# The third pair of heads projected one tile at a time, and a straighter pace for attention

## The chip, the cores and the metric

One core of a Trainium2 chip runs the whole kernel. Its engines are TensorE (PE; its weight loads are PEld), VectorE (DVE), ScalarE (ACT), GpSimd (POOL) and SyncE (SP, which here only issues DMAs). Each engine works through its own list of instructions, and they wait for each other by semaphores. The metric is the device time of the kernel in microseconds (us), the median of several executions; lower is better. A profile is one execution recorded instruction by instruction.

## The reference, cut to what matters

An encoder block: a normalised input goes through one input projection, whose columns feed a Mamba-2 branch (z, xBC, dt) and an attention branch (q, k, v); both are normalised, projected out, and followed by a SwiGLU feed-forward.

```
h = rms_norm(x, pre_mix_gain)                    # 1024 rows x 1024
z, xbc, dt_raw, q, k, v = split(h @ w_in)
xbc = silu(causal_depthwise_conv(xbc))           # -> ssd_scan(...) * silu(z), group rms_norm
# stick-breaking attention, 8 heads of 64, strictly causal
log_1mb = log_sigmoid(-z);  after = reverse exclusive cumsum(log_1mb)
w = exp(log_sigmoid(z) + after);  o = w @ v      # rms_norm per head
x = x + rms_norm(concat(y_ssd, y_sb) @ w_out)
x = x + rms_norm((silu(h2 @ w_gate) * (h2 @ w_up)) @ w_down)
```

## The kernel before, in words

Every large product is made as three matmuls (`mm3`, lines 78 to 80): operands are split in a high and a low part (`split`, line 74 a cast on ACT, line 75 a subtraction on DVE), and high x high, low x high and high x low are summed in PSUM. A tile of the input projection is 128 columns of `w_in` against all 1024 rows: two halves of 512 rows, each 8 x 3 matmuls of 128x512, 48 in all (`proj`, names `pj_q`, `pj_k`, `pj_v`, `pj_x`, `pj_z`). Heads go in pairs: one q, one k and one v tile for two heads; pair 0 is made before the stage of this case, pairs 1, 2 and 3 are `qkv1`, `qkv2`, `qkv3`. The eight x tiles (`conv_tile`) are scaled into `u` (line 375) and convolved by `taps` (line 384 three times and line 387 once, on DVE).

In the stage of this case two streams are merged into one program: attention (a list of 32 units: pair, head, two blocks of 128 queries) and the fill (the projection tiles in the order of `PLAN`, with `taps` and the chunked scan `ssd` as side work between their steps). Each step of a stream states costs, PE time for the fill and DVE time for attention. The merge compares attention's share of its total with a curve over the fill's share and lets the one that is behind go on:

```
x = min(f / F_ALL * 8, 7.99)
pace = PACE[int(x)] + (x - int(x)) * (PACE[int(x) + 1] - PACE[int(x)])
if not da and (db or (not stall and a / A_ALL <= pace)):
    c = next(ga, None)
```

So `PACE` has nine points, one for each eighth of the fill. A scheduler then orders each engine's list; an engine takes its list in order.

A unit of attention: `zp` (line 565 and 566, q against high and low k), two sigmoids on ACT into `sn` and `sp` (lines 567 and 568), a select on POOL (line 570), on DVE a running product (`sn`, line 571) and a product (`sp`, line 572), four transposes a piece on PE (`tp`, line 582), the cast `wh` on ACT and the rest `wl` on DVE (lines 586, 587), and the product with v (`o`, line 594). After the last unit of a pair its output is squared on ACT and summed on PE (`nps`, line 491).

Before attention's first sigmoids ACT makes eight decay tiles `ab` (line 362; each comes from a DMA, a POOL select in line 360 and a DVE subtraction in line 361) and, after the last of them, the scales that the sigmoids take (lines 366 and 367). v of pair 0 is transposed on PE (`pv`) and copied (`vv`, line 549 on ACT, line 550 on DVE). The weights of a tile are fetched from DRAM in two halves of 256 KB (`wr`, line 168) some matmuls into the tile before, and split into `wh` and `wl`; two raw buffers and four split ones are shared by all tiles.

Of the kernel before, what the change touches and what calls it, by code (L numbers as in the profile page):

```python
# [32 lines left out]
EPS = 1e-6  # L33
NEG = -1e30

PLAN = ('qkv1', 'x0', 'x1', 'x2', 'x3', 'x4', 'x5', 'qkv2', 'x7', 'x6', 'ssd', 'qkv3', 'z0', 'z1', 'r0', 'z2', 'z3', 'wo', 'l1', 'o0')

PACE = (-0.109, 0.104, 0.264, 0.337, 0.474, 0.601, 0.751, 0.876, 1.027)
A_ALL, F_ALL = 146.4, 259.0
SIDE = 1  # L40
URGENT = 150
# [7 lines left out]
def tile_hybrid_block(  # L49
# [20 lines left out]
    last_mm, evac, last_dve = [None], [None], [None]  # L70
# [6 lines left out]
    def mm3(ps, ah, al, bh, bl, start, stop, more=False):  # L77
        T.matmul(ps, lhsT=ah, rhs=bh, start=start, stop=False, skip_group_check=more)  # L78
        T.matmul(ps, lhsT=ah, rhs=bl, start=False, stop=False, skip_group_check=more)  # L79
        last_mm[0] = T.matmul(ps, lhsT=al, rhs=bh, start=False, stop=stop, skip_group_check=more)  # L80
# [9 lines left out]
    def psum(tag, name, shape=None, dt=F32):  # L90
        return psP.tile(shape or [P, 512], dt, tag=tag, name=name, bufs=BANKS[tag])
# [81 lines left out]

    ORDER = [f"{k}{t[3]}" if t[:3] == "qkv" else t for t in PLAN if t[0] in "qxz" for k in ("qkv" if t[0] == "q" else "x")]
    START = {"q": COL_Q, "k": COL_K, "v": COL_V, "x": COL_XBC, "z": COL_Z}
    cols = [(n, START[n[0]] + P * int(n[1])) for n in ["q0", "k0", "v0"] + ORDER]
    w_tiles = {}

    def fetch_w(half=None):

        if cols:
            name, col = cols[0]
            w = w_tiles.setdefault(name, [])
            for dh in range(2) if half is None else (half,):
                w.append(load_w_half(col, name, dh))
            if len(w) == 2:
                cols.pop(0)

    def w_of(w, d):
        hi, lo = w[d // 4]
        return hi[:, d % 4, :], lo[:, d % 4, :]
# [5 lines left out]
    with tc.tile_pool(reuse_waits="tile", name="xp", bufs=4, side="left") as xp:  # L199
# [5 lines left out]
        for d in range(ND):  # L205
            t = xp.tile([P, S], F32, tag="xt", name=f"xt{d}")
# [38 lines left out]
    def proj(name, evac, dve):  # L245
        if name not in w_tiles:
            fetch_w()
        w = w_tiles.pop(name)
        for n in range(2):
            ps = psum("mm", f"pj_{name}")  # L250
            for d in range(ND):
                mm3(ps, *w_of(w, d), hh[d][n], hl[d][n], d == 0, d == ND - 1)
                if n == 0 and d in (3, 5):
                    fetch_w(d // 2 - 1)
                if d % 2 and d < ND - 1:
                    yield 1.3, 0
            evac(n, ps, slice(512 * n, 512 * n + 512))
            yield 1.3, dve

    def qkv_tiles(j, st):  # L260


        def store(key, n, i, t):
            nc.sync.dma_start(qkv_d[j][key][i][:, 512 * n : 512 * n + 512], t)

        def two(key, n, src):
            hi, lo = [t2.tile([P, 512], F32R, tag="t2", name=key + x) for x in "hl"]
            split(hi, lo, src)
            store(key, n, 0, f32(hi))
            store(key, n, 1, f32(lo))  # L270

        def evac_q(n, ps, sl):
            two("q", n, ps)
            st["q"] = n == 1

        def evac_k(n, ps, sl):
            kr = t2.tile([P, 512], F32, tag="t2", name="kr")
            V.tensor_tensor(kr, ps, R_b[:, sl], ALU.mult)
            two("k", n, kr)
            st["k"] = n == 1  # L280

        def evac_v(n, ps, sl):
            vr = t2.tile([P, 512], F32, tag="t2", name="vr")
            V.tensor_tensor(vr, ps, R_b[:, sl], ALU.mult)
            if j == 0:
                v_first.append(vr)
            else:
                store("v", n, 0, vr)
            if n == 1:
                st["v"] = True  # L290

        return evac_q, evac_k, evac_v

    v_first = []

    def proj_qkv(j, st):
        for key, evac in zip("qkv", qkv_tiles(j, st)):
            yield from proj(f"{key}{j}", evac, {"q": 0.6, "k": 1.2, "v": 0.6}[key])


    def dt_stage():
# [68 lines left out]
    def conv_tile(c):  # L370
        u = big.tile([P, S + 3], F32, tag="u", bufs=2, name=f"u{c}")
        G.memset(u[:, S : S + 3], 0.0)

        def evac(n, ps, sl):
            V.tensor_tensor(u[:, sl], ps, R_b[:, sl], ALU.mult)

        yield from proj(f"x{c}", evac, 0.6)

        def taps():
            y = big.tile([P, S], F32, tag="G", name=f"cy{c}")  # L380
            sg = big.tile([P, S], F32, tag="dec", name=f"csg{c}")
            A.activation(y, u[:, 3 : 3 + S], AF.Identity, scale=cw[:, 0, c : c + 1], bias=cb[:, c : c + 1])
            for j in (1, 2, 3):
                V.scalar_tensor_tensor(y, u[:, 3 - j : 3 - j + S], cw[:, j, c : c + 1], y, ALU.mult, ALU.add)
                yield 0, 1.2
            A.activation(sg, y, AF.Sigmoid)
            V.tensor_tensor(y, y, sg, ALU.mult)
            nc.sync.dma_start(cx_d[c], y)
            yield 0, 1.1

        side.append(taps())
# [268 lines left out]
    def merge(ga, gb):  # L660
# [3 lines left out]
        while not (da and db):  # L664
# [3 lines that stand above are left out]
# [10 lines left out]
    st = [dict() for _ in range(4)]  # L678
# [33 lines left out]
    wo = rpA = None  # L712
# [94 lines left out]
    def stage(t):  # L807
        nonlocal wo
        if t[:3] == "qkv":
            yield from proj_qkv(int(t[3]), st[int(t[3])])  # L810
        elif t[0] == "x":
            yield from conv_tile(int(t[1]))
        elif t == "ssd":
            side.append(ssd())
            yield 0, 0.1
        elif t[0] == "z":
            if t == "z0":
                yield from flush()
            yield from z_tile(int(t[1]))
        elif t == "wo":  # L820
            right_h.close()
            wo = es_w.enter_context(tc.tile_pool(reuse_waits="tile", name="wo", bufs=1, side="right"))
            out_load(0, "early")
            raws = fetch_wo()
            yield 0, 3
            yield from load_wo(raws)
            rows_rstd(1, 1, t2, tag="t2")
            yield 0, 1
        elif t == "r0":
            rows_rstd(1, 0, t2, tag="t2")  # L830
            yield 0, 1
        elif t == "o0":
            yield from out_mm(0, "early")
        elif t == "l1":
            out_load(1, "early")
            yield 0, 3

    def fill():
        for t in PLAN:
            for c in stage(t):  # L840
# [494 lines left out]
    for i in range(n_all):  # L1335
        while len(steps) <= min(i + AHEAD, n_all - 1):
            steps.append(prep(len(steps)))
        q, p = "1267543"[i // NP], i % NP
        if p == 0 and q in "1675":
            banks[q] = [bank("pd") for _ in range(4)]  # L1340
        if q == "3" and p >= NP - TAIL:
# [3 lines left out]
            for b in range(4):  # L1345
                for t in range(TAIL - 1, -1, -1):
                    mms(i - t, b)
                t = temp()
# [10 lines left out]
        for b in range(4):  # L1359
# [15 lines left out]
            elif q == "4":  # L1375
                t = temp()
# [44 lines left out]
```

## Time and profile before

| | us |
|---|---|
| median of 3 runs | 1226.1 (1224.39 to 1229.47) |
| the profiled execution's own time | 1223.84 |
| its span, first to last instruction | 1222.1 |
| PE busy | 1186.1 (97%) |
| DVE busy | 929.8 (76%) |
| ACT busy | 585.3 (48%) |

"Busy" is the union of an engine's instructions; a matmul that waits for its operands inside the pipeline counts as busy, so a busy PE isn't PE at its peak. The profiled execution lies 2.26 us under the median, and its span 1.74 us under its own time.

### The profile page before, as it was taken

Reading aid. Unit: us, or ns where it says so; the run is one execution under the profiler, and the core shown is the slowest. Engines: PE = TensorE matmul, PEld = TensorE weight load, DVE = VectorE, ACT = ScalarE, POOL = GpSimd, SP = SyncE. Lnnn points to the kernel's source line nnn. Section 1 sums busy time; section 2 is a strip of 40 time slices with the busy share of each in tenths; the row PEclk is TensorE's granted clock in tenths of the full one; section 3 lists DMA queues with packets and bytes.
Section 4 is the critical chain, followed back from the end, with each engine's and each line's share of the span. In section 5 each row is a group of like instructions: output and inputs, shape, how many; then the busy total and the mean of one; then the engine's idle time right before and its main releaser. Section 6 shows DMA issues by size and latency. Waiting matters only on the chain.

```text
span 1222.1 us, 16315 instructions
## 1 busy us (share of the span) xinstructions
PE 1186.1 (97%) x5641; PEld 966.0 (79%) x5641; DVE 929.8 (76%) x1461; ACT 585.3 (48%) x1115; POOL 92.6 (8%) x232
## 2 busy tenths in 40 slices
PE   9998999999999998999999999999999999999997
PEld 7776778887887776788788888888888888888885
DVE  7478988769997978668898755566555558998877
ACT  7347655546654776446653323333233335444453
POOL 0041110010100100011200000000000000000000
PEclk9999999999999999999999999999999999999999
DMA  6793342345657424767973322322223298233346
GB/s 192 198 341 111 92 134 91 118 118 172 180 151 221 137 79 155 227 191 221 314 207 110 104 77 79 104 69 87 78 78 104 96 334 285 69 122 100 114 136 236
DMA packets 141994, 184.27 MB, mean 151 GB/s; under 512 B 10724, under 2 KB 96964, under 8 KB 141912
## 3 DMA queue, kind: packets, MB, share of 16 engines
q1 hardware_dynamic: 130656, 152.23, 40.8%
q0 software_dynamic: 7424, 25.17, 5.5%
q10 hardware_dynamic: 3832, 5.84, 1.3%
q8 instruction: 44, 0.72, 0.3%
q14 instruction: 38, 0.31, 0.1%
HBM read 133.28 MB, written 49.92 MB: 150 GB/s over the span
## 4 chain that ended last, share of the span: by engine, by line
PE 72%; DVE 13%; DMA 5%; ACT 5%; issue 4%; SPq 1%; DVEq 0%; ACTq 0%
PE pd L79 5%; PE pd L78 5%; PE pd L80 5%; DVE sn L571 3%; DMA Rb<-r_d 2%; PE o L594 2%; PE tp L582 2%; PE pj_x L78 2%; PE pj_x L80 2%; PE pcu L80 2%; PE pcg L80 2%; PE peu L80 2%; PE peg L80 2%; PE peu L79 2%; PE peg L79 2%
## 5 line engine op out<-in xcount | busy, mean ns | idle before, releaser
L74 ACT CAST flhi<-fraw 128x512 fp32r<-128x512 f32 x98 | 60.3, 621 | 153.5 <-PE pcg L79 35.6
L79 PE MATMUL pd<-folo,fohi 128*128 128x512 f32 x260 | 101.4, 390 | 0.0
L80 PE MATMUL pd<-fohi,folo 128*128 128x512 f32 x260 | 101.2, 389 | 0.0
L78 PE MATMUL pd<-fohi 128*128 128x512 f32 x260 | 101.2, 389 | 0.0
L571 DVE TENSOR_TENSOR_SCAN sn<-sn,smask 128x1024 f32<-128x1024 f32 (+3 forms) x64 | 87.3, 1365 | 17.6 <-ACT sn L567 17.4
L75 DVE TENSOR_TENSOR fllo<-fraw,flhi 128x512 fp32r<-128x512 f32 x98 | 66.7, 684 | 29.2 <-ACT flhi L74 29.2
L567 ACT ACTIVATE sn<-zp,msc 128x512 f32<-128x512 f32 (+2 forms) x96 | 56.0, 585 | 34.5 <-PE zp L566 28.9
L74 ACT CAST fohi<-rt 128x512 fp32r<-128x512 f32 x83 | 48.5, 618 | 45.6 <-PE pd L79 22.9
L586 ACT CAST wh<-tp 128x512 fp32r<-128x512 f32 (+1 forms) x80 | 42.7, 544 | 38.5 <-PE tp L582 38.0
L74 ACT CAST flhi<-fs 128x512 fp32r<-128x512 f32 x44 | 27.3, 622 | 69.5 <-PE peg L79 34.5
L75 DVE TENSOR_TENSOR folo<-rt,fohi 128x512 fp32r<-128x512 f32 x83 | 54.9, 687 | 7.3 <-ACT fohi L74 7.3
L587 DVE TENSOR_TENSOR wl<-tp,wh 128x512 fp32r<-128x512 f32 (+1 forms) x80 | 49.7, 628 | 10.8 <-ACT wh L586 10.3
L79 PEld LDWEIGHTS pd<-folo,fohi 128*128 128x128 f32 x260 | 48.8, 188 | 10.6 <-DVE folo L75 0.6
L568 ACT ACTIVATE sp<-zp,msc 128x512 f32<-128x512 f32 (+2 forms) x96 | 55.9, 585 | 2.5 <-PE tp L582 2.4
L78 PEld LDWEIGHTS pd<-fohi 128*128 128x128 f32 x260 | 48.8, 188 | 10.2
L80 PEld LDWEIGHTS pd<-fohi,folo 128*128 128x128 f32 x260 | 48.8, 188 | 10.1
L582 PE MATMUL tp<-ident,sp 128*128 128x128 f32 x288 | 48.0, 278 | 5.7 <-DVE sp L572 5.1
L78 PE MATMUL po<-woh,yhl 128*128 128x512 f32 x128 | 50.5, 395 | 2.6 <-ACT yhl L74 2.2
L1015 POOL DMA_DIRECT2D a_d<-sg x44 | 23.9, 542 | 376.8 <-DVE sg L1014 376.8
L78 PE MATMUL pj_x<-hh,wh_x 128*128 128x512 f32 x128 | 52.2, 408 | 0.0
L80 PE MATMUL pj_x<-hh,wl_x 128*128 128x512 f32 x128 | 51.0, 398 | 0.0
L80 PE MATMUL po<-woh,yhl 128*128 128x512 f32 x128 | 50.1, 393 | 0.5 <-DVE yhl L75 0.5
(425 smaller groups left out, 3457.6 us busy)
## 6 DMA issues: line engine op xcount, KB each, us to landing
ps<-a_d SPq DMA_DIRECT2D x55, 256.0 KB
fraw<-in_w_gate_dram SPq DMA_DIRECT2D x22, 512.0 KB
fraw<-in_w_up_dram SPq DMA_DIRECT2D x22, 512.0 KB
a_d<-sg POOLq DMA_DIRECT2D x44, 256.0 KB, 2.6
rt<-in_w_down_dram SPq DMA_DIRECT2D x33, 256.0 KB
rt<-a_d SPq DMA_DIRECT2D x22, 256.0 KB
ps<-in_w_down_dram SPq DMA_DIRECT2D x22, 256.0 KB
xt<-in_x_t_dram SPq DMA_DIRECT2D x8, 512.0 KB
```

The costliest lines, as they stand in the source:

```text
L74: A.copy(hi, src)
L75: V.tensor_tensor(lo, src, f32(hi), ALU.subtract)
L78: T.matmul(ps, lhsT=ah, rhs=bh, start=start, stop=False, skip_group_check=more)
L79: T.matmul(ps, lhsT=ah, rhs=bl, start=False, stop=False, skip_group_check=more)
L80: last_mm[0] = T.matmul(ps, lhsT=al, rhs=bh, start=False, stop=stop, skip_group_check=more)
L567: A.activation(sn[:, 1 + off : 1 + off + cw_], zp[:, 0:cw_], AF.Sigmoid, scale=rqn[:, qb : qb + 1])
L568: A.activation(sp[:, off : off + cw_], zp[:, 0:cw_], AF.Sigmoid, scale=rqp[:, qb : qb + 1])
L571: V.tensor_tensor_scan(sn[:, 1 : 1 + W], sn[:, 1 : 1 + W], smask[:, 0:W], 1.0, ALU.mult, ALU.max)
L582: T.transpose(tp[:, P * i : P * i + P], ws[a][:, co : co + P], ident)
L586: A.copy(wh[:, 0:n_], tp[:, 0:n_])
L587: V.tensor_tensor(wl[:, 0:n_], tp[:, 0:n_], f32(wh[:, 0:n_]), ALU.subtract)
L594: T.matmul(o[:, 0:cw_], lhsT=vv[:, k, h, :], rhs=wt[:, c0 : c0 + cw_], start=(first and k == kb + 1 and wt is wh), stop=(last and k == kb ...
```

## The change

`PLAN` has no `qkv2` any more: `q2`, `k2` and `v2` stand one by one, `q2` behind `x0`, `k2` behind `x2`, `v2` behind `x4`. `proj_qkv` takes the letters to make, `stage` and `ORDER` (the order in which weights are fetched) know the single tiles. The first five points of `PACE` change, the last four stay.

```diff
-PLAN = ('qkv1', 'x0', 'x1', 'x2', 'x3', 'x4', 'x5', 'qkv2', 'x7', 'x6', 'ssd', 'qkv3', 'z0', 'z1', 'r0', 'z2', 'z3', 'wo', 'l1', 'o0')
+PLAN = ('qkv1', 'x0', 'q2', 'x1', 'x2', 'k2', 'x3', 'x4', 'v2', 'x5', 'x7', 'x6', 'ssd', 'qkv3', 'z0', 'z1', 'r0', 'z2', 'z3', 'wo', 'l1', 'o0')
-PACE = (-0.109, 0.104, 0.264, 0.337, 0.474, 0.601, 0.751, 0.876, 1.027)
+PACE = (-0.14, 0.06, 0.195, 0.33, 0.465, 0.601, 0.751, 0.876, 1.027)
...
-    ORDER = [f"{k}{t[3]}" if t[:3] == "qkv" else t for t in PLAN if t[0] in "qxz" for k in ("qkv" if t[0] == "q" else "x")]
+    ORDER = [f"{k}{t[3]}" if t[:3] == "qkv" else t for t in PLAN if t[0] in "qkvxz" for k in ("qkv" if t[:3] == "qkv" else "x")]
...
-    def proj_qkv(j, st):
+    def proj_qkv(j, st, keys="qkv"):
         for key, evac in zip("qkv", qkv_tiles(j, st)):
-            yield from proj(f"{key}{j}", evac, {"q": 0.6, "k": 1.2, "v": 0.6}[key])
+            if key in keys:
+                yield from proj(f"{key}{j}", evac, {"q": 0.6, "k": 1.2, "v": 0.6}[key])
...
+        elif t[0] in "qkv":
+            yield from proj_qkv(int(t[1]), st[int(t[1])], t[0])
```

Three places where it moves instructions. First ACT's list at the start of attention, from the last decay tiles to the first sigmoid. Before:

```order
L549 CAST vv_925<-pv 128x8x64
L362 ACTIVATE ab<-ab 128x1024
L74 CAST kh<-kr 128x512
L549 CAST vv_925<-pv 128x8x64
L74 CAST wh_x_949<-wr_x_947 128x512
L74 CAST wh_x_986<-wr_x_984 128x512
L362 ACTIVATE ab<-ab 128x1024
L366 ACTIVATE msc<-msc 128x8
L367 ACTIVATE msc<-msc 128x8
L567 ACT_TABLE_LOAD
L567 ACTIVATE sn<-zp,msc 128x512
```

The same place of the changed kernel (its line numbers are one higher from here on):

```order
L363 ACTIVATE ab<-ab 128x1024 x4
L74 CAST kh<-kr 128x512
L74 CAST wh_x_892<-wr_x_890 128x512
L74 CAST wh_x_929<-wr_x_927 128x512
L74 CAST wh_q_1066<-wr_q_1064 128x512
L363 ACTIVATE ab<-ab 128x1024
L367 ACTIVATE msc<-msc 128x8
L368 ACTIVATE msc<-msc 128x8
L550 CAST vv_971<-pv 128x8x64
L568 ACT_TABLE_LOAD
L568 ACTIVATE sn<-zp,msc 128x512
```

The first half of q2's weights (`wh_q_1066`) now stands ahead of the last decay tile, and a `vv` cast between the scales and the table load.

Second PE's list in the second unit of attention, whose transposes are `tp`, beside x0's projection (`pj_x_1133` and `pj_x_1253` are its halves before, `pj_x_1129` its second half now). Before:

```order
L582 MATMUL tp<-ident,sp 128x128 x8
L565 MATMUL zp<-kh,qq 128x256
L594 MATMUL o<-wh,vv_925 128x256
L566 MATMUL zp<-kl,qq 128x256
L594 MATMUL o<-wl,vv_925 128x256
L594 MATMUL o<-wh,vv_925 128x128
L594 MATMUL o<-wl,vv_925 128x128
L594 MATMUL o<-wh,vv_925 128x256
L582 MATMUL tp<-ident,sp 128x128
L565 MATMUL zp<-kh,qq 128x128
L566 MATMUL zp<-kl,qq 128x128
L78 MATMUL pj_x_1253<-hh_1_203,wh_x_949 128x512
```

And now:

```order
L583 MATMUL tp<-ident,sp 128x128 x2
L80 MATMUL pj_x_1129<-hh_1_207,wl_x_893 128x512
L78 MATMUL pj_x_1129<-hh_1_209,wh_x_892 128x512
L79 MATMUL pj_x_1129<-hl_1_210,wh_x_892 128x512
L80 MATMUL pj_x_1129<-hh_1_209,wl_x_893 128x512
L78 MATMUL pj_x_1129<-hh_1_211,wh_x_929 128x512
L79 MATMUL pj_x_1129<-hl_1_212,wh_x_929 128x512
L80 MATMUL pj_x_1129<-hh_1_211,wl_x_930 128x512
L78 MATMUL pj_x_1129<-hh_1_213,wh_x_929 128x512
L79 MATMUL pj_x_1129<-hl_1_214,wh_x_929 128x512
L80 MATMUL pj_x_1129<-hh_1_213,wl_x_930 128x512
L583 MATMUL tp<-ident,sp 128x128 x4
```

Where eleven rows of attention followed each other, ten matmuls of the projection now stand between two groups of transposes.

Third PE's list where the first pair of heads ends, marked by its first `nps` (x3's halves are `pj_x3_1778` the second, before, and `pj_x3_1892` the first, now). Before:

```order
L80 MATMUL pj_x3_1778<-hh6_1_215,wl_x3_1553 128x512
L78 MATMUL pj_x3_1778<-hh7_1_217,wh_x3_1552 128x512
L79 MATMUL pj_x3_1778<-hl7_1_218,wh_x3_1552 128x512
L80 MATMUL pj_x3_1778<-hh7_1_217,wl_x3_1553 128x512
L491 MATMUL nps_1814<-nsq_1812,sel2_95 2x512
L78 MATMUL pj_x4_1849<-hh0_0_187,wh_x4_1734 128x512
```

And now:

```order
L78 MATMUL pj_x3_1892<-hh3_0_193,wh_x3_1741 128x512
L79 MATMUL pj_x3_1892<-hl3_0_194,wh_x3_1741 128x512
L80 MATMUL pj_x3_1892<-hh3_0_193,wl_x3_1742 128x512
L492 MATMUL nps_1921<-nsq_1919,sel2_95 2x512
L78 MATMUL pj_x3_1892<-hh4_0_195,wh_x3_1778 128x512
L79 MATMUL pj_x3_1892<-hl4_0_196,wh_x3_1778 128x512
```

Before, pair 0 ended behind x0 to x3, 192 projection matmuls after `qkv1`; now it ends behind x0, q2, x1, x2, k2 and a quarter of x3, 252 of them. The second pair's `nps` stand within six projection matmuls of where they were (the start of `qkv3`), and from there on both lists hold the same work in nearly the same order.

## Rows read from the trace of the kernel before

**Rows 1.** The page's first part: busy time of each engine, its share of the span, and instructions.

```profile
PE 1186.1 (97%) x5641; PEld 966.0 (79%) x5641; DVE 929.8 (76%) x1461; ACT 585.3 (48%) x1115; POOL 92.6 (8%) x232
```

**Rows 2.** Busy time by stretch of the span: first pair of heads (98 to 179 us), second pair (179 to 287), then to the end of the merged stage (about 510). Columns: stretch and its length, then PE, PEld, DVE, ACT, POOL busy us (instructions), granted clock, DMA share, GB/s.

```profile
98.00:179.00 81.00, 74.70 (x391) 61.03 (x391) 76.40 (x92) 52.62 (x99) 11.69 (x39) 0.98 0.33 88
179.00:287.00 108.00, 105.97 (x545) 88.03 (x546) 85.66 (x107) 59.51 (x109) 9.97 (x34) 1.00 0.41 121
287.00:400.00 113.00, 110.60 (x676) 91.58 (x675) 100.31 (x153) 63.15 (x139) 10.33 (x39) 1.00 0.61 181
400.00:510.00 110.00, 102.77 (x499) 75.81 (x498) 86.16 (x131) 71.97 (x132) 6.09 (x20) 1.00 0.45 146
```

**Rows 3.** The same view in finer stretches; the last number but two is the granted clock.

```profile
99.30:102.80 3.50, 3.50 (x12) 2.57 (x11) 3.30 (x3) 2.33 (x5) 0.71 (x2) 0.51 0.00 0
102.80:125.00 22.20, 19.70 (x118) 15.76 (x118) 21.45 (x31) 16.68 (x36) 3.84 (x14) 1.00 0.33 87
125.00:150.00 25.00, 23.27 (x123) 19.25 (x122) 24.26 (x29) 15.95 (x28) 2.11 (x8) 1.00 0.31 82
150.00:179.00 29.00, 26.92 (x140) 22.45 (x138) 26.55 (x32) 16.37 (x30) 4.81 (x14) 1.00 0.38 100
200.00:250.00 50.00, 48.56 (x254) 40.96 (x254) 39.42 (x51) 27.71 (x51) 4.62 (x18) 1.00 0.39 118
```

**Rows 4.** What PE waited for from 60 to 290 us: PE's tile and line, whose instruction released it, us in total, times, the longest.

```profile
PE tp L582 <- DVE sp L572: 4.2, 5, 1.4
PE zp L565 <- ACT sp L568: 3.5, 1, 3.5
PE o L594 <- DVE wl L587: 2.4, 6, 0.7
PE pj_v L78 <- DVE kr L278: 1.6, 1, 1.6
PE nps L491 <- ACT nsq L488: 1.5, 1, 1.5
```

**Rows 5.** PE's instructions in order of time: start, us, line, tile; in brackets the idle time before it and what ended it. The first two are the first and the last of 30 projection matmuls that follow each other without a gap.

```profile
67.25 0.39 PE L78 MATMUL pj_k<-hh,wh_k 128*128 128x512 f32 x1
...
73.83 0.39 PE L80 MATMUL pj_k<-hh,wl_k 128*128 128x512 f32 x1
...
87.22 0.50 PE L78 MATMUL pj_v<-hh,wh_v 128*128 128x512 f32 x1 [1.58 <-DVE kr L278]
...
97.90 0.50 PE L565 MATMUL zp<-kh,qq 128*128 128x512 f32 x1 [3.52 <-ACT sp L568]
```

**Rows 6.** ACT's instructions before the first sigmoids, as in rows 5.

```profile
86.89 1.06 ACT L362 ACTIVATE ab<-ab 128x1024 f32<-128x1024 f32 x1
...
88.36 0.59 ACT L549 CAST vv<-pv 128x512 fp32r<-128x512 f32 x1
88.84 1.15 ACT L74 CAST wh_x<-wr_x 128x512 fp32r<-128x512 f32 x2
94.01 1.06 ACT L362 ACTIVATE ab<-ab 128x1024 f32<-128x1024 f32 x1 [4.03 <-DVE ab L361]
...
95.28 1.28 ACT L567 ACT_TABLE_LOAD   x1
96.58 0.69 ACT L567 ACTIVATE sn<-zp,msc 128x512 f32<-128x512 f32 x1
```

**Rows 7.** DVE, POOL and SP in the same stretch, as in rows 5.

```profile
76.95 5.07 DVE L75 TENSOR_TENSOR kl<-kr,kh 128x512 fp32r<-128x512 f32 x1 [1.03 <-ACT kh L74]
...
77.25 4.22 POOL L360 TENSOR_SCALAR_AFFINE_SELECT ab<-ab 128x1024 f32<-128x1024 f32 x4
...
86.49 0.68 DVE L278 TENSOR_TENSOR kr<-pj_k,R_b 128x512 f32<-128x512 f32 x1
...
88.49 1.95 DVE L75 TENSOR_TENSOR kl<-kr,kh 128x512 fp32r<-128x512 f32 x1 [0.73 <-ACT kh L74]
...
88.78 1.11 POOL L360 TENSOR_SCALAR_AFFINE_SELECT ab<-ab 128x1024 f32<-128x1024 f32 x1
...
90.47 0.34 SPq L264 DMA_DIRECT2D k_d<-kl  x1
```

**Rows 8.** Two transfers of 256 KB, the size of half a tile's weights: from the page's list of DMAs (issues, KB each, median us from issue to landing), and from the chain of waits (start, us).

```profile
a_d<-sg POOLq DMA_DIRECT2D x44, 256.0 KB, 2.6
...
83.64 3.75 DMA kh<-k_d
```

**Rows 9.** Groups of instructions by line and shape, 179 to 287 us: count, busy us, mean ns, idle before. The two `tp` rows are of 98 to 179 us and of 179 to 287 us.

```profile
L582 PE MATMUL tp<-ident,sp 128*128 128x128 f32 x72 | 12.3, 280 | 2.3 <-DVE sp L572 2.3
...
L582 PE MATMUL tp<-ident,sp 128*128 128x128 f32 x72 | 11.7, 275 | 1.9 <-DVE sp L572 1.9
...
L75 DVE TENSOR_TENSOR wl_q<-wr_q,wh_q 128x512 fp32r<-128x512 f32 x4 | 2.7, 677 | 0.0
...
L278 DVE TENSOR_TENSOR kr<-pj_k,R_b 128x512 f32<-128x512 f32 x2 | 1.4, 685 | 2.6 <-PE pj_k L80 2.6
...
L75 DVE TENSOR_TENSOR ql<-pj_q,qh 128x512 fp32r<-128x512 f32 x2 | 1.4, 680 | 0.0
L75 DVE TENSOR_TENSOR kl<-kr,kh 128x512 fp32r<-128x512 f32 x2 | 1.4, 680 | 0.1
L550 DVE TENSOR_TENSOR vv<-pv,vv 128x512 fp32r<-128x512 f32 x2 | 1.4, 688 | 0.0
```

## The prediction

> **What bounds the kernel now.** I read the page's first part first: PE is busy 97% of the span [rows 1]. All PE work stays the same with this change, so it can only win or lose time in which PE stands still, runs at a lower clock, or waits inside its pipeline. Next I cut the span by the work of attention, because both kernels do the same attention in each cut: the first pair of heads from 98 to 179 us and the second to 287 us [rows 2]; each has 72 rows of transposes [rows 9]. The first stretch has DVE at 76.4 of 81 us (94%) and PE idle for 6.3; the second has DVE at 85.7 of 108 us (79%) and PE idle for 2.0 [rows 2]. So before, DVE has hardly any slack while the first pair runs, and PE waits for it; the releasers say the same: products on DVE ahead of the transposes, 4.2 us, and the rests `wl` ahead of the product with v, 2.4 us [rows 4].
>
> Idle time isn't the whole loss. Thirty projection matmuls in a row start at 67.25 and the last at 73.83, so 6.58/29 = 0.227 us each [rows 5]. The second stretch holds 545 - 391 = 154 more PE instructions than the first [rows 2]; taken as projection matmuls they need 35.0 us, but the stretch is only 27 us longer. The first stretch thus loses **8.0 us more** than the second with the same attention. Of these, 4.3 are idle time (6.3 - 2.0), and about 1.7 the clock: from 99.3 to 102.8 us the granted clock is 0.51, half of full speed, 1.2 instead of 2.4 GHz, and 3.5 us at half speed cost 1.7 [rows 3]. It comes behind PE's longest wait of the stage, 3.52 us to 97.90 [rows 5]. The other 2.0 are waits inside the pipeline.
>
> **The start of attention.** What "begins later" buys is small, because the first sigmoids are not held back by their place. PE's first `zp` results lie ready, but ACT makes the last decay tile at 94.01, having idled 4.03 us for DVE's subtraction, then the scales, a table load of 1.28 us, and the first sigmoid at 96.58 [rows 6]; the fifth `zp` needs a PSUM bank that these free [rows 4, 5]. The changed order leaves that chain in place and puts two things into it. (a) The first half of q2's weights is cast ahead of the last decay tile. Its DMA stands behind the store of `kl`, at 90.47 before [rows 7], and needs the raw buffer that x0's weights free one 0.68-us subtraction later [rows 9]: issue at about 90.9. A transfer of this size takes 2.6 to 3.75 us [rows 8], so it lands at 93.5 to 94.65, and the 0.58-us cast (half of the 1.15 of two [rows 6]) ends at 94.1 to 95.2: the last decay tile moves from 94.01 by 0.1 to 1.2 us. (b) A `vv` cast of 0.59 us [rows 6] now stands between the scales and the table load. So the first sigmoid comes 0.7 to 1.8 us later. Against that PE has three more projection matmuls behind it when the fifth `zp` must wait (eight of x0's instead of five), 0.7 us. PE's wait for `kr`, to 87.22 [rows 5], ends at the same time, since DVE makes that `kr` at 86.49 in the same place of its list [rows 7]; the eight `pv` transposes that PE used to do ahead of it come after it, and count as done in both at the fifth `zp`. **Term: 0 to +1.2 us, I take +0.5**, nearer to the fast end, because the median of 44 transfers is 2.6 and the 3.75 is a single one among many others. The clock's dip I leave where it is, since a wait of about the same length stands ahead of it.
>
> On (a) the Trainium skill has a rule ("TensorE: Matmul & The Clock Gate", the table at its head): ScalarE works through a strict first-in, first-out queue. The trace agrees as far as it goes: ACT idles 4.03 us for one decay tile while `zp` results wait [rows 6]. By the rule (a) costs its 0.1 to 1.2 us; if ACT could pass the cast over, the term would be about 0 instead of +0.5.
>
> **The middle.** Pair 0 used to end 192 projection matmuls behind `qkv1` and now ends 252 behind it, pair 1 where it did within six. So 60 x 0.227 = 13.6 us of PE work move from the second stretch into the first: 94.6 and 94.4 us at the old losses. DVE's work moves less. By the order, the first stretch gets q2's and k2's evacuations (two `ql`, two `kr`, two `kl`, 6 x 0.68 = 4.1 us), two more weight halves (1.4) and one `vv` (0.7), and gives up one `u` and one `vr` (1.4); the convolutions of x0, x1 and x2, twelve instructions, are in it both times. The durations are those of the groups [rows 9]. DVE then has 76.4 + 4.8 = 81.2 of 94.6 us (86%) in the first stretch and 85.7 - 4.8 = 80.9 of 94.4 us (86%) in the second.
>
> What does a stretch lose at 86%? The two rows known are 79% (the base) and 94% (8.0 us above it). On a straight line 85.8% is 0.43 of the way from 79.3 to 94.3: 3.5 us each, 7.0 for both, a gain of 1.0. If waits grow as the square of the way (DVE's idle time is what absorbs a late piece, and it runs out at the end), it is 0.19: 1.5 each, 3.0 for both, a gain of 5.0. The finer rows lean to a curve: PE idles 2.5 us in 22.2 and 1.7 in 25 with DVE at 97%, but 1.4 in 50 with DVE at 79% [rows 3]. But the clock's 1.7 and the first unit's waits are tied to the start and stay. **Term: -1.0 to -5.0 us, I take -2.5.**
>
> **What moves at no cost.** The transfers of q2, k2 and v2's weights stand on SP between x tiles now, each a tile ahead of use; no wait of PE from 60 to 290 us ended with a projection's weights, and that is the cover [rows 4]. If it is gone, half a tile costs at most a transfer, 2.6 to 3.75 us [rows 8]. q2, k2 and v2 are ready earlier for pair 2, so its loads can't come late. From `qkv3` on both lists hold the same work in nearly the same order; PE idles 2.4 us up to 400 and 7.2 up to 510 [rows 2], and a reshuffle there can give or take part of it: **0, bounds -1.5 and +1.5.**
>
> **Sum.** +0.5 - 2.5 + 0 = -2.0 us. The profiled execution took 1223.84 us, its span 1222.1, so these become 1221.8 and 1220.1; the median of the runs shown is 2.3 higher, and from 1226.1 the forecast is **1224.1 us**. The terms' ends give -6.5 to +1.7, 1219.6 to 1227.8.
>
> **The rivals.** *A clear gain.* The dense start is the whole cause: with projection matmuls between the pieces of the first units, PE reaches each piece after DVE has made it, the square law holds (-5.0), the dip of the clock goes (-1.7) and the start costs nothing: -6.7, 1219.4; with the later stage falling well, 1218. For it speaks that ten projection matmuls stand where there were none; against it that the fifth `zp` waits for the same decay chain, so the wait ahead of the dip stays [rows 5, 6].
>
> *It doesn't do what it says.* Losses follow the straight line, since DVE's work is only moved (-1.0), and the later sigmoids take it back (+1.2): +0.2, 1226.3. With a bad reshuffle behind it, 1228. For it: the total of DVE's work is unchanged, and half of the first stretch's excess is waits on single pieces [rows 4] that a mean share doesn't describe.
>
> *Slower: the second stretch becomes the dense one.* Attention must catch up in it. Its price starts where DVE's work there reaches what it had in the first stretch, 94% of 94.4, or 88.9 us, 8.0 us above my count: then it loses the 8.0 that the first one gave up, and with 1.5 to 3.5 still lost in the first and +0.5 at the start the kernel is 2.0 to 4.0 us slower, about 1229; above that each us of DVE work costs one, and 1232.2, the bound of slower, needs 92 to 94. What could lengthen DVE's work is POOL: a `kl` that takes 0.68 us took 5.07 beside POOL's selects [rows 7, 9]. But POOL is busy only 10.0 us in that whole stretch [rows 2], so even all of it laid on DVE would give 90.9. The Trainium skill says of such pairs ("SBUF — State Buffer", Who interferes with whom) that a DVE instruction with two inputs in SBUF and a GpSimd instruction that reads SBUF block each other fully; the row agrees with it.
>
> **How the numbers follow.** Forecast, 0.3 to 6 us faster: 0.52. Clear gain, over 6 us: 0.21. No change or up to 6 us slower: 0.18. Slower by more: 0.09. Half a per cent of 1226.1, 6.1 us, is about what a measurement of this kernel can tell from no change; so faster 0.21, same 0.70, slower 0.09. The forecast's own range is 1220 to 1226. For 8 in 10 I go into the clear gain down to 1217.0 and into the loss up to 1229.5, leaving out a tenth on either side.
>
> **What would show it.** In the new trace: the first sigmoid 0.7 to 1.8 us later than 96.58 and PE's wait ahead of the fifth `zp` still 3 to 4 us; a stretch at half clock behind it; the end of the first pair (the cut at 179) about 12 us later and that of the second (the cut at 287) about 2 us earlier; DVE at 84 to 88% in both stretches; PE's idle time in both together down from 8.3 to 5 or 6 us; from 290 us on the old waits at the old sizes. I am wrong if the first stretch's waits stay although DVE has slack there (then single chains set them, not DVE's share), if the second stretch has DVE above 92%, or if the difference arises behind `qkv3`.

## The result, and the profile after

The changed kernel took **1231.06 us** (median of 15 executions, 1227.05 to 1232.73), the kernel before 1226.1: ratio **1.0033, 95% interval 1.0025 to 1.0041**, so about 4 us slower. The forecast was 1224.1 with a range of 1217.0 to 1229.5. The profiled execution of after took 1231.39 us, its span 1229.7.

The page's first part, which answers [rows 1]:

```profile
PE 1191.8 (97%) x5641; PEld 967.8 (79%) x5641; DVE 929.7 (76%) x1461; ACT 586.5 (48%) x1115; POOL 89.6 (7%) x232
```

The same instructions, and PE busy for 5.7 us more: most of what this execution lost is not idle time, but PE at a lower clock or waiting inside its pipeline. The stretches that answer [rows 2], first cut by the clock as forecast (first pair to 192, second to 292, then the rest of the merged stage), and the first two once more from the fifth `zp` to the first `nps` of each pair, the same work in every kernel within a few instructions:

```profile
98.00:192.00 94.00, 86.90 (x448) 71.20 (x448) 81.28 (x99) 60.37 (x112) 10.41 (x39) 0.98 0.38 109
192.00:292.00 100.00, 95.58 (x495) 77.55 (x493) 83.59 (x104) 57.06 (x102) 9.12 (x36) 1.00 0.38 104
292.00:408.00 116.00, 113.59 (x684) 92.77 (x682) 99.16 (x153) 64.25 (x143) 10.78 (x39) 1.00 0.59 174
408.00:517.00 109.00, 100.11 (x476) 72.75 (x475) 83.31 (x126) 68.97 (x124) 5.42 (x19) 0.98 0.46 148
...
101.44:192.28 90.84, 87.18 (x449) 71.20 (x449) 80.27 (x98) 56.96 (x105) 9.86 (x38) 0.98 0.37 104
192.28:292.26 99.98, 95.56 (x494) 77.55 (x494) 83.57 (x105) 57.13 (x102) 9.12 (x36) 1.00 0.38 104
```

DVE stands at 86% and 84%, about as forecast (81.2 and 80.9 us were counted, 81.28 and 83.59 came). The first stretch did get better: PE idles 90.84 - 87.18 = 3.7 us in it instead of 6.3 [rows 2]. The second gives it back, 99.98 - 95.56 = 4.4 instead of 2.0. Together 8.1 against 8.3, where 5 or 6 was forecast. The first pair ends about 13 us later than before, as forecast; the second, forecast 2 us earlier than 287.60, ends 4.7 us later, at 292.26.

PE's waits from 60 to 292 us, answering [rows 4] (PE's tile and line, releaser, us in total, times, the longest):

```profile
PE tp L583 <- DVE sp L573: 5.8, 10, 1.1
PE zp L566 <- ACT sp L569: 3.7, 1, 3.7
PE pj_v L78 <- DVE kr L278: 2.5, 1, 2.5
PE o L595 <- DVE wl L588: 1.1, 3, 0.6
```

The wait of `nps` (1.5) is gone and that of `o` is down from 2.4 to 1.1; the transposes wait ten times instead of five. At the start of attention ACT's list, answering [rows 6] (start, us, line, tile, in brackets the idle time before and what ended it):

```profile
88.80 1.13 ACT L74 CAST wh_x<-wr_x 128x512 fp32r<-128x512 f32 x2
96.56 0.62 ACT L74 CAST wh_q<-wr_q 128x512 fp32r<-128x512 f32 x1 [6.63 <-DMA wr_q<-in_w_in_dram]
97.09 1.05 ACT L363 ACTIVATE ab<-ab 128x1024 f32<-128x1024 f32 x1
...
98.83 1.28 ACT L568 ACT_TABLE_LOAD   x1
100.12 0.69 ACT L568 ACTIVATE sn<-zp,msc 128x512 f32<-128x512 f32 x1
```

and SP's issue of that transfer, answering [rows 7]:

```profile
91.50 0.91 SPq L168 DMA_DIRECT2D wr_q<-in_w_in_dram  x1
```

ACT stands still for 6.63 us for half a tile's weights: issued at 91.50, used at 96.56, 5.06 us. The DMA share (last column but one) of the stretches around it is full:

```profile
86.00:91.50 5.50, 3.55 (x10) 2.86 (x11) 4.47 (x6) 3.78 (x6) 2.85 (x6) 0.69 1.04 354
91.50:96.60 5.10, 5.10 (x28) 4.27 (x27) 2.31 (x3) 0.04 (x1) 0.20 (x2) 1.00 1.04 360
```

The same view of before had shown it:

```profile
86.00:91.00 5.00, 3.78 (x16) 3.11 (x17) 4.27 (x6) 3.98 (x7) 2.47 (x6) 1.00 1.00 375
91.00:96.00 5.00, 3.38 (x14) 2.17 (x12) 2.98 (x5) 1.97 (x4) 0.75 (x3) 1.00 0.97 318
```

A full share alone doesn't make 5.06 us: the 3.75-us transfer of [rows 8] had a share of 0.97 beside it (before). But that one was issued ahead of the stores of the decay tiles, and q2's half comes right behind them: in after four stores `dec_d` of 512 KB each were issued from 85.28 to 88.67, with a median of 5.2 us to landing. First the stretch of before, then the first and the last of these issues in after:

```profile
83.64:87.39 3.75, 2.17 (x10) 1.49 (x9) 3.75 (x5) 3.61 (x5) 1.62 (x3) 1.00 0.97 274
...
85.28 0.55 POOL L364 DMA_DIRECT2D dec_d<-ab  x1 [3.08 <-ACT ab L363]
...
88.67 0.53 POOL L364 DMA_DIRECT2D dec_d<-ab  x1 [0.60 <-ACT ab L363]
```

That the half waits for these stores to drain is argued from this; no run takes them away.

PE's answer to [rows 5]: the wait ahead of the fifth `zp` is where it was in length, 3.67 us, and the one for `kr` grew from 1.58 to 2.52.

```profile
87.95 0.80 PE L78 MATMUL pj_v<-hh,wh_v 128*128 128x512 f32 x1 [2.52 <-DVE kr L278]
...
101.44 0.80 PE L566 MATMUL zp<-kh,qq 128*128 128x512 f32 x1 [3.67 <-ACT sp L569]
```

Around the end of both a stretch at half clock begins, as in two other places of this execution (granted clock, last number but two; answers [rows 3]):

```profile
49.70:53.10 3.40, 3.40 (x10) 2.59 (x9) 0.82 (x3) 0.26 (x1) 0.00 (x0) 0.52 0.79 195
87.20:90.60 3.40, 2.65 (x6) 2.16 (x7) 2.37 (x3) 2.65 (x5) 2.31 (x5) 0.53 0.99 352
101.10:104.50 3.40, 3.06 (x8) 2.58 (x9) 2.30 (x2) 2.71 (x5) 0.63 (x2) 0.51 0.29 114
510.70:514.10 3.40, 2.88 (x7) 2.30 (x8) 2.23 (x8) 2.43 (x5) 0.00 (x0) 0.51 0.95 324
```

By an estimate each costs up to 1.7 us, 3.4 us at half speed, and less where PE would have waited anyway. The one at 49.7 lies ahead of everything that the change touches; e6 and e10, which are the kernel before up to there, have it too. So the two profiled executions differ by 7.6 us where the medians differ by 5 and the ratio says 4: totals below are ratios over many executions, and single profiles are only compared inside marked stretches, with their slow pieces counted.

### The profile page after: what moved, and what is told of

It reads as the page before. It is cut to its first block, busy times and chain, and to the rows that moved or that the text cites. A ratio compares the mean times of both kernels' runs of the same rounds, so it can differ in the third digit from the quotient of the medians.

```text
span 1229.7 us, 16311 instructions
## 1 busy us (share of the span) xinstructions
PE 1191.8 (97%) x5641; PEld 967.8 (79%) x5641; DVE 929.7 (76%) x1461; ACT 586.5 (48%) x1115; POOL 89.6 (7%) x232
## 4 chain that ended last, share of the span: by engine, by line
PE 71%; DVE 11%; issue 7%; DMA 5%; ACT 4%; SPq 1%; POOL 1%; ACTq 0%; DVEq 0%; POOLq 0%
PE pd L79 5%; PE pd L80 5%; PE pd L78 5%; DVE sn L572 3%; PE tp L583 2%; PE peu L79 2%; PE peg L79 2%; PE pcu L79 2%; PE pcg L79 2%; PE peu L78 2%; PE peg L78 2%; PE pcu L78 2%; PE pcg L78 2%; PE pcg L80 2%; PE peu L80 2%
## 5 line engine op out<-in xcount | busy, mean ns | idle before, releaser
L79 PE MATMUL pj_x<-hl,wh_x 128*128 128x512 f32 x128 | 50.8, 397 | 0.0
```

## The experiments

Ratios are to the kernel before on the same chip, with 95% intervals. The marks are of the profiled execution: the fifth `zp` (and PE's wait ahead of it), the first `nps` of the second pair, and a wait of 1.55 us for `nsq` near the end of the stage that all kernels have ("late mark"). The difference of two ratios is good to about 0.0014, or 1.7 us. "Single chain" below means a sequence of instructions on several engines that each wait for the one before, as opposed to an engine that has too little idle time.

| kernel | ratio | fifth `zp` (wait) | second pair's `nps` | late mark | `zp` to late mark |
|---|---|---|---|---|---|
| before | 1 | 97.90 (3.52) | 287.60 | 475.41 | 377.5 |
| after | 1.0033 | 101.44 (3.67) | 292.26 | 481.93 | 380.5 |
| e1_q2_late | 1.0017 | 97.14 (0.41) | 288.37 | 478.30 | 381.2 |
| e4_p4_only | 1.0023 | 96.93 (3.51) | 288.15 | 477.68 | 380.8 |
| e5_late_474 | 0.9985 | 98.23 (1.78) | 286.58 | 475.62 | 377.4 |
| e9_after_474 | 1.0004 | 99.69 (3.52) | 287.35 | 474.95 | 375.3 |
| e14_again_474 | 0.9986 | 97.29 (1.77) | 285.46 | 473.29 | 376.0 |

**e1_q2_late: the cast of q2's first weight half behind the last decay tile.** The last decay tile's instruction is kept, and the split waits for its place in the list:

```diff
-        split(hi, lo, raw)
+        with tc.issue_after(last_ab[0].ins) if name == "q2" and dh == 0 else nullcontext():
+            split(hi, lo, raw)
```

> The changed kernel (1231.1), with one thing put back: the cast of q2's first weight half stands behind the last decay tile on ACT instead of ahead of it. Theory of the start (a cast that waits for a transfer stands ahead of the decay chain in an in-order queue; in the changed kernel's trace that transfer lasts from 91.5 to 96.5 us and the first sigmoid comes at 100.1 instead of 96.6): the first sigmoid comes back to 97 to 98, the wait ahead of the fifth zp to 1 to 2 us, and the time falls by 1.5 to 3 us to 1228 to 1229.5. Rival (the start is absorbed later, since the rest of the first pair is bound elsewhere): the sigmoid comes back, the time stays at 1231.

Measured: 1228.77 us, ratio 1.0017 (1.0006 to 1.0028). ACT's list there (the same view as above):

```profile
92.78 1.06 ACT L364 ACTIVATE ab<-ab 128x1024 f32<-128x1024 f32 x1 [0.41 <-DVE ab L363]
...
95.82 0.69 ACT L569 ACTIVATE sn<-zp,msc 128x512 f32<-128x512 f32 x1
```

The 6.63 us are gone and the granted clock behind the fifth `zp` is full:

```profile
97.10:100.50 3.40, 3.36 (x14) 2.38 (x14) 2.60 (x2) 3.24 (x6) 0.89 (x2) 1.00 0.47 183
```

PE's wait ahead of the fifth `zp` shrinks from 3.67 to 0.41 us. So the place of this one cast costs 0.0016, 2.0 us; but it is only half of the loss.

**e2_plan_only and e3_pace_only: the two tables apart.** The changed program with the old pace, and with the old list and the new pace.

> The kernel before with the new PLAN alone (q2, k2, v2 one by one; the old PACE). The start of attention is that of before, so the theory of the start expects the first sigmoid at 96.6. If the tiles' order is what costs in the middle, 1228 to 1230; if it is the pace (the theory of the catch-up: attention is moved behind 180 us and DVE, loaded more there, makes PE wait), 1225 to 1227.

> The kernel before with the new PACE alone (qkv2 in one piece behind x5). Theory of the start and of the catch-up: 1229 to 1232, with a weights' cast ahead of the last decay tile here too and the first sigmoid 2 to 3.5 us later. Rival (the tiles' order costs): 1226.

Measured: 1226.46 us, 1.0009 (0.9994 to 1.0024), and 1233.53, 1.0057 (1.0042 to 1.0071). The list alone does nothing that can be told from no change; the pace does the harm, more than the 1229 to 1232 us expected of it, and the list takes back some 3 us. e3 shows that the stall at the start isn't q2's: with the old list it is x1's first weight half that a later start puts ahead of the last decay tile, and ACT waits longer still.

```profile
97.57 0.62 ACT L74 CAST wh_x<-wr_x 128x512 fp32r<-128x512 f32 x1 [7.29 <-DMA wr_x<-in_w_in_dram]
```

**e4_p4_only: one point of the pace.**

```diff
-PACE = (-0.109, 0.104, 0.264, 0.337, 0.474,
+PACE = (-0.109, 0.104, 0.264, 0.337, 0.465,
```

> The kernel before with one number of PACE changed, the fifth, 0.474 to 0.465. Up to the fourth eighth of the fill its order is that of before, from qkv3 on that of the changed kernel. In the trace of the changed kernel 3 to 3.5 us of the loss come behind qkv3. If the order there costs (the late theory): 1228 to 1230, the loss behind 290 us. If the loss there is only chance of that one profile or the clock's dips: 1226, no difference.

Measured: 1228.98 us, 1.0023 (1.0013 to 1.0033). 0.009 in the fifth point costs the kernel before 2.8 us, and PE's list is unchanged up to about 221 us.

**e5_late_474 and e9_after_474: start and fifth point, crossed.** e5 is e1 with the fifth point back at 0.474, e9 is the changed kernel with that point alone put back.

> The changed kernel with q2's first cast put behind the last decay tile, and with the fifth point of the pace back at 0.474. Theory of separate terms: the start costs +2.0 us and the late order that the fifth point makes +2.8; with both undone the middle's -0.75 is left, so 1225.5 us (ratio 0.9994, 0.998 to 1.001), and PE's waits from 290 to 510 us are those of the kernel before. Rival: the late loss comes from the thinner start of attention (it has to be caught up whatever the fifth point says); then the ratio stays at 1.0017 (1228.8 us).

> The changed kernel with the fifth point of the pace alone back at 0.474, q2's first cast where the change put it. If start, middle and late order add up: 1.0033 less the 0.0032 between e1_q2_late and e5_late_474, so 1.0001 (0.999 to 1.001), 1226.4 us; the first sigmoid stays near 100 us. Rival: the late loss is only there with the early start of e1 and of the kernel before, and the ratio stays at 1.0033.

Measured: e5 1224.4 us, 0.9985 (0.9975 to 0.9995); e9 1226.95, 1.0004 (0.9994 to 1.0014). Within these intervals the two edits add up: the cast costs 0.0016 at 0.465 (after less e1) and 0.0019 at 0.474 (e9 less e5), the point 0.0032 (e1 less e5) and 0.0029 (after less e9). What the point does is seen between the last two marks, `nps` and the late mark:

```profile
287.35 1.02 PE L492 MATMUL nps<-nsq,sel 128*2 128x512 f32 x2
...
474.95 1.02 PE L492 MATMUL nps<-nsq,ones_f 128*1 128x512 f32 x2 [1.55 <-ACT nsq L489]
```

187.6 us in e9, and in after

```profile
292.26 1.02 PE L492 MATMUL nps<-nsq,sel 128*2 128x512 f32 x2
...
481.93 1.02 PE L492 MATMUL nps<-nsq,ones_f 128*1 128x512 f32 x2 [1.55 <-ACT nsq L489]
```

189.7. By the table this stretch takes 187.6 to 187.8 us in before, e9 and e14, and 189.5 to 189.9 in after, e1 and e4, with no slow piece of the clock in any of them: about 2 us. It is not the same in every execution: e5, the same program as e14, took 189.0, and 1.2 us of that is one wait for a transfer (`cx`); e8, also with 0.474, took 189.8, with PE idle for 7.2 us of it. What repeats is where the time of the new order goes: into the 148 matmuls `o` and the 88 `zp` in this stretch. Busy PE time of these two tiles alone, `o` first, in before and in e4:

```profile
287.60:475.41 187.81, 28.78 (x148) 1.00 0.48 147
287.60:475.41 187.81, 22.73 (x88) 1.00 0.48 147
288.15:477.68 189.53, 29.94 (x148) 1.00 0.48 145
288.15:477.68 189.53, 23.61 (x88) 1.00 0.48 145
```

In all seven kernels with 0.474 and full convolutions (before, e2, e5, e7, e8, e9, e14) `o` takes 28.8 us and `zp` 22.7 to 22.8; in all four with 0.465 (after, e1, e3, e4) 29.9 to 30.0 and 23.6 to 23.7. So the same matmuls of attention take 2 us longer in the other order, without PE being idle; what they wait for inside PE stays open.

Before this stretch, the point acts already in that of the second pair. e9 (fifth `zp` to the first pair's `nps`, and on to the second's):

```profile
99.69:190.53 90.84, 87.38 (x449) 71.37 (x449) 80.28 (x98) 57.09 (x105) 9.90 (x38) 0.98 0.37 104
190.53:287.35 96.82, 93.95 (x488) 76.56 (x487) 81.85 (x102) 56.02 (x101) 11.57 (x35) 1.00 0.39 107
```

Here PE idles 2.9 us in the second stretch; with 0.465 it was 4.4, and the `nps` came six instructions later. From the fifth `zp` to the second `nps`, e9 needs 187.7 us and before 189.7, with one slow piece at the start in each; e9 has three projection matmuls fewer to do there (0.7 us), which stand ahead of its fifth `zp`.

**e6_before_483, e12_late_470, e13_late_478: the fifth point at other values,** the first on the kernel before, the others on e5.

> The kernel before with the fifth point of the pace at 0.483 instead of 0.474. If the late loss of 0.465 comes from more attention left beside the scan, more attention done ahead of it gains about as much: -2.8 us, 1223.5 (ratio 0.9977). If 0.474 only happens to fall well and any shift reshuffles waits, it is 0 to +3 us (ratio 1.000 to 1.0025).

> e5_late_474 with the fifth point of the pace at 0.470, between the 0.465 of e1_q2_late (ratio 1.0017) and the 0.474 of e5_late_474 (0.9985). If the late loss grows with the attention left beside the scan, it is in between: about 1.000 (0.999 to 1.001). If each shift falls into another order with waits of its own, anything from 0.9985 to 1.003, not in line with the distance.

> e5_late_474 with the fifth point at 0.478, on the other side. If less attention beside the scan is better, 0.997 to 0.998. If 0.474 falls well by chance, as e6_before_483 (1.0044) says for the kernel before, 0.999 to 1.003.

Measured: 1231.05 us, 1.0044 (1.0028 to 1.0060); 1226.99, 1.0012 (1.0002 to 1.0022); 1231.28, 1.0045 (1.0030 to 1.0060). On e5's base 0.465, 0.470, 0.474, 0.478 give 1.0017, 1.0012, 0.9985, 1.0045; on the kernel before 0.465, 0.474, 0.483 give 1.0023, 1, 1.0044. Both values above 0.474 cost more than any reading had expected of them (at most 1.0025 and 1.003). So the loss doesn't follow the amount of attention left beside the scan: it rises on both sides of one value. In e13 part of it is visible as waits that e14 doesn't have at this length, the `nps` of finished pairs from 285 to 475 us and a z tile:

```profile
PE nps L493 <- ACT nsq L490: 2.9, 2, 2.3
PE o L596 <- DVE wl L589: 1.8, 4, 0.6
PE pj_z L78 <- DVE zr L510: 0.8, 1, 0.8
```

At 0.465 no single wait stands out: from the second pair's `nps` to the late mark PE idles 6.0 us in after and 5.4 in before. The rest lies in busy time: the 2 us of the longer `o` and `zp`, less what the six instructions done earlier took.

**e7_late_steep and e8_late_between: the points in the middle.** Both have e1's start and 0.474. e7 has the old third and fourth points (0.264, 0.337), e8 has 0.215 and 0.35.

> q2's first cast behind the last decay tile, the new list, the first two points of the new pace (attention begins later) and the third to fifth of the old: attention catches up within the second eighth of the fill. If a dense stretch loses by its density wherever it lies, the first pair's stretch is dense again and what it gave up is lost: 1226 to 1227 us (ratio 1.000 to 1.0007), with PE's idle time up to the first nps at 4 us or more. If the first stretch gains by its projection matmuls between the first units' pieces alone, that gain stays and the second stretch no longer has to catch up: 1222.5 to 1224 (0.997 to 0.998).

> As e5_late_474, but with the third and fourth points of the pace at 0.215 and 0.35 instead of 0.195 and 0.33: attention half an eighth less behind in the middle. If the second stretch loses because it must catch up, the loss there (PE idle 4.4 us in the changed kernel) falls to 2 to 3 us and the time lies 1 to 2 us under e5_late_474, 1224. If waits there are single chains that the density does not set, it is within 1 us of e5_late_474.

Measured: e7 1225.5 us, 0.9994 (0.9980 to 1.0008); e8 1231.24, 1.0036 (1.0024 to 1.0049). e7's first stretch is as the first theory said: with attention caught up early the first pair is dense again (DVE 71.1 of 79.2 us, 90%), and PE idles 6.5 us. Its time lies between the two that were expected, and its interval reaches both.

```profile
98.78:178.00 79.22, 72.70 (x388) 58.80 (x389) 71.11 (x86) 51.90 (x99) 12.47 (x38) 1.00 0.37 100
```

e8 went against both theories: 0.02 in two points costs 6 us against e5. Two of its largest waits, from 187 to 290 us, are single ones, of 2.1 us ahead of the first pair's `nps` and of 2.2 for an `sp`; its first stretch is no denser than e14's (DVE 88% in both), yet PE idles 8.1 us in it against 4.7.

```profile
PE tp L584 <- DVE sp L574: 3.9, 4, 2.2
PE nps L493 <- ACT nsq L490: 2.1, 1, 2.1
```

**e10_before_light and e11_474_light: less DVE work.** The kernel before, and e5, with the three products of `taps` on 64 of 1024 columns, so that the convolution's result is incomplete:

```diff
-                V.scalar_tensor_tensor(y, u[:, 3 - j : 3 - j + S], cw[:, j, c : c + 1], y, ALU.mult, ALU.add)
+                V.scalar_tensor_tensor(y[:, 0:64], u[:, 3 - j : 67 - j], cw[:, j, c : c + 1], y[:, 0:64], ALU.mult, ALU.add)
```

> The kernel before with the three convolution products on DVE (taps) cut to 64 of 1024 columns: 24 instructions of 1.27 us shrink, eleven of them up to the end of the first pair; the convolution's result is incomplete, the order of PE's list stays. If DVE's share sets the first stretch's loss, PE's idle time from the first sigmoids to the first nps (6.3 us in 81 before) falls to 4 or less, and the time by 3 to 6 us. If chains through ACT, POOL and DVE set it, piece by piece, it stays at 5 to 6.3 and the time falls by 0 to 2.

> e5_late_474 with the same cut in the taps. If DVE's share makes the second stretch give back the first one's gain, PE's idle time from the first nps to 292 us (4.2 in e5_late_474) falls to 2 or less and the time by 3 to 6 us below e5_late_474; against e10_before_light there is then little left to gain (within 1 us). If single chains do it, the idle time stays at 3 to 4 and the distance to e10_before_light stays at about -1.9 us.

Measured: e10 1223.16 us, 0.9980 (0.9970 to 0.9990); e11 1222.59, 0.9968 (0.9956 to 0.9981). First pair in e10, from the fifth `zp`, and PE's waits around it:

```profile
99.08:178.34 79.26, 75.22 (x392) 62.35 (x392) 69.29 (x93) 53.19 (x99) 10.13 (x39) 0.96 0.34 91
```

```profile
PE zp L565 <- ACT sp L568: 3.5, 1, 3.5
PE tp L582 <- DVE sp L572: 2.2, 3, 1.3
PE o L594 <- DVE wl L587: 1.6, 4, 0.5
```

DVE at 87% instead of 94%, PE idle 4.0 us instead of the 6.4 between the same marks of before, and 2.5 us saved in all by the ratio, between what the two readings expected. The waits for `nsq` and `wl` gave way; of the transposes' 2.3 us in this stretch 2.2 stayed. e11's second pair:

```profile
188.78:288.00 99.22, 95.87 (x495) 77.59 (x495) 73.34 (x106) 57.97 (x104) 9.53 (x36) 1.00 0.37 105
```

DVE falls from 84% to 74% there and PE still idles 3.35 us (e14: 3.1). So less DVE work relieves PE where DVE stands at 94% and not where it stands at 84%. Between, the share alone says little: at 87 to 88% PE idles 3.5 us in the first stretch of e9, 4.0 in e10's, 4.7 in e14's and 8.1 in e8's. As a whole e11 is 0.0017 under e5, 2.1 us; where it gains them was not followed up.

**e14_again_474: the best version once more.**

> e5_late_474 once more, unchanged, beside the two others: 0.9985 (0.9975 to 0.9995) again if it really is ahead of the kernel before; 1.000 if that was the luck of its executions.

Measured: 1223.09 us against 1225.41, ratio 0.9986 (0.9974 to 0.9997). The changed list and pace with one cast moved and one point put back is ahead of both kernels, by 1.7 us of the kernel before, twice measured. Its two stretches idle 4.7 and 3.1 us, more than e9's, but there is no slow piece of the clock up to 1218 us, and from the matmul that the wait for `kr` releases (86.10 in e9, 87.04 here) PE reaches its fifth `zp` 3.3 us earlier.

## Why the prediction was wrong, point by point

The sign was wrong and the time is outside the range. Its three terms, +0.5, -2.5 and 0, against what the runs say:

**The late stage, 0 with bounds of 1.5, is the step that failed most: +2.8 to +3.9 us** (e4; after less e9; e1 less e5). I took "the same work in nearly the same order" for a cover and drew the bounds from a share of PE's idle time [rows 2]. But the fifth point changes the order at hundreds of places between about 220 and 470 us, and what it costs shows little as idle time: the same `o` and `zp` take 2 us longer. Every other value tried cost 2.8 to 7.4 us, on either side: 0.474 is a narrow minimum in a stage where waits of 1 to 2 us come and go with the order. The prediction did name it among what would make it wrong ("the difference arises behind `qkv3`") and put a bad reshuffle into its second rival, at 1228; it sized neither from anything that the order does. Why the matmuls of attention take longer in the new order stays open.

**The start, +0.5 with bounds 0 and 1.2, came to +2.1.** Marks by the clock hide it, since each execution reaches this place at a time of its own. Counted from the matmul that the wait for `kr` releases (87.22 before, 87.95 after), the first sigmoid comes 9.36 us later in before, 12.17 in after and 12.27 in e9: 2.8 to 2.9 us later than before, where 0.7 to 1.8 was forecast. The three projection matmuls gained are worth the 0.7 us that was counted for them. The mis-sized term is the transfer: 2.6 to 3.75 us were taken from transfers at other places [rows 8], and it took 5.06, behind the decay stores. The prediction looks neither at the DMA share of this stretch nor at the stores issued just ahead. The effect of the order of ACT's list was as stated: ACT idles 6.63 us ahead of a cast while a decay tile and the sigmoids stand behind it. The Trainium skill's rule ("TensorE: Matmul & The Clock Gate", the table at its head) that ScalarE takes its queue strictly first in, first out agrees with this. With the cast moved, the first sigmoid comes after 8.9 us (e1, e5, e14), earlier than in before, so the 2.0 to 2.3 us that the cast costs against e1 and e5 are not the same quantity as this term, though they are about as large.

**The middle, -2.5, went the way forecast in e9 alone, and less far.** e9 needs 2.0 us less from the fifth `zp` to the second `nps`, 1.3 if the three matmuls already done are given back; PE's idle time there is 3.5 + 2.9 = 6.3 against 8.3 (5 or 6 was forecast); DVE's shares came out about as counted. In the changed kernel itself 1.5 us of idle time are back in the second stretch, because the fifth point already acts there. In e14 the whole stretch takes 188.2 us, 1.5 less than before, and before has a slow piece in it that e14 hasn't: with the cast moved, no gain of the middle itself is left to see. Nor is the curve that I chose over the straight line shown: e9 lies nearer to the curve, e14 nearer to the line.

What I left out altogether is the clock at both waits. I noted that a slow piece follows the 3.52-us wait and left it where it is. In all eight profiles with a wait of 3.5 us or more ahead of the fifth `zp` (before, after, e2, e3, e4, e6, e9, e10) the granted clock drops to about 0.5, 1.2 GHz, within 1.7 us of the wait's end, and in none of the eight with a wait of 0 to 1.8 us (e1, e5, e7, e8, e11, e12, e13, e14). So a shorter wait can save the piece too. Its 1.7 us, an estimate, are about as much as e5's whole gain over the kernel before (1.8 us), but no run takes the piece away and leaves the wait. At `kr` the new pace brings PE there earlier: the wait grew from 1.5 to 1.9 us (five profiles with the old pace, none followed by half clock) to 2.4 to 2.8 (eleven with the new, six followed by it). In after and e9 the longer wait for the fifth `zp` follows that slow piece and can hide it, so its cost can't be read off. That the eight `pv` transposes count as done in both was right.

**The sum.** In the prediction's own terms it is +2.1 (start) - 1.3 (middle) + 2.9 x 1.226 = 3.6 (late stage), 4.4 us, beside the measured 4.05 (3.1 to 5.0). The first two are read from single profiles, so this agrees as far as such readings go. The ratios of e5, e9 and after give -1.8, then +2.3 for the cast and +3.6 for the point; they add up to the measured loss by construction and prove nothing further.

**The rivals.** "It doesn't do what it says" came closest: a middle of -1.0 that the later sigmoids take back, 1226.3, is nearly what e9 shows (-1.3 and +2.2 in its profile; 1226.95 measured). Its bad reshuffle is the fifth point, at about twice the 1.7 us that separate its 1228 from its 1226.3. "Slower" came true in sign but not by its mechanism: DVE reached 84% in the second stretch, far from 92. The "clear gain" rested on the dip going away when the wait ahead of it does; that mechanism exists, but this change didn't shorten the wait, e1's edit does.

## What to carry to other kernels

Before a cast or a load is priced, read the DMA share of its own stretch and what was issued just ahead of it: here 5.06 us behind four stores, 3.75 ahead of them. A cast that waits for its transfer holds up what stands behind it on ACT (6.63 us here). A table that orders a stage has a reach from the changed point to the end of that stage; price the re-ordering by what other values of the same point do (here 3 to 7 us for steps of 0.004 to 0.02), not by the idle time that the old order shows. Time a stage from a mark in the work and not by the clock. And cross two suspected parts (with and without each): where each costs the same with and without the other, within the intervals, they are two causes.

## What the runs showed of the hardware

Most of the 3.4-us pieces at half clock begin at or behind a wait of PE of 1 to 4 us, at the start of attention, around 244 (e6, 2.1 us) and around 510 us (after, 2.5 us), and the same wait is followed by one in some executions and not in others. The one near 49.7 us comes without any: PE in after is busy for all of the 9.7 us ahead of it, at full clock.

```profile
40.00:49.70 9.70, 9.70 (x58) 8.33 (x57) 3.97 (x8) 4.06 (x6) 0.00 (x0) 1.00 0.56 172
```

It stands in after, e2, e3, e5, e6, e7, e10, e11 and e12, and not in before, e1, e4, e8, e9, e13 and e14, all with the same work there. One program was profiled twice: e5 has this piece and e14 hasn't, and their spans differ by 3.1 us, of which the piece is 1.7 at most by the estimate above. In three profiles (e2, e3, e10) the piece behind the fifth `zp` lasted twice as long, 6.8 us.
